# Element-wise work on SBUF operands moved from GpSimd to VectorE in a two-layer diffusion trunk

## The chip, the core and the metric

The program runs on one core of one Trainium2 chip, in one launch. The metric is the device time of one execution in microseconds, as a median over runs. The engines are TensorE (PE, matrix products), VectorE (DVE), ScalarE (ACT), GpSimd (POOL) and SyncE (SP, which only issues transfers). Each engine takes its own instructions strictly in order and waits on semaphores of the others.

## The reference: what is computed

Two layers of a trunk over 640 tokens (128 context tokens and 512 latent tokens) with 1024 channels, in float32. Each layer is: a normed and modulated copy of x, a token mixer, an output projection with a gated residual, a second norm, a SwiGLU feed-forward part of 2816 hidden units, and a second gated residual.

```python
for l in range(DEPTH):
    sh1, sc1, g1, sh2, sc2, g2 = split(silu(cond) @ ada_w[l] + ada_b[l], 6)
    h = rmsnorm(x, norm1_w[l]) * (1 + sc1) + sh1
    y, st = mixer_ab(h) if l % 2 == 0 else mixer_c(h)
    x = x + g1 * y
    h = rmsnorm(x, norm2_w[l]) * (1 + sc2) + sh2
    x = x + g2 * swiglu(h)
```

Layer 0's mixer is a chunked gated delta rule in two directions (convolution, SiLU and an l2 norm over q and k ahead of it, an RMS norm behind it) beside a grouped-query attention. Layer 1's mixer is a bidirectional chunked mLSTM. The states, the new keys and values, and y are returned.

## The kernel before

Activations lie transposed: 128 channels on the partitions, 640 tokens along the free axis, in 8 tiles. Every large product is made of three passes over fp32r operands: a number is split into a high part (a cast, on ACT) and a low part (the number less its high part), and the passes are high x high, high x low and low x high. So each weight block that arrives has a low part made once, and so has each activation tile.

The order of the work is this, with the times of the profiled execution:

- 0 to 60 us, `ada_start`: the modulation vectors of layer 0 come from row sums on DVE (`ada_tile`, L323). For each of 8 tiles of x a list (`START`) runs the row sums (`sc_in`), the sum of squares (`Norm.square`, L237) and the scaled split (`Norm.scale`, L217 to L223).
- 60 to 176 us, in `layer0`: 12 products `conv` (PE at L508, tile qkv). Behind each stand a 5-tap convolution on DVE (L980, four `scalar_tensor_tensor` on 644 elements), a SiLU on ACT (L984, tile kq or vy) and PE transposes of it (L992). Row sums of later modulation vectors (`ada_fill`, L323) are put in between. `Norm.finish` (L267, L269, L271) makes the normed activations, `bias_b` adds a bias to the gates and to z, and `after_k`, `after_q` make factors of the l2 norms.
- 176 to 430 us: the attention and the scan. `finish(c)` norms the output of each of five chunks.
- 412 to 500 us, `out_half` twice: 8 products of 24 matmuls each, the residual (`resid`, L558), and in the second one the scaled split and sum of squares of the next norm, with a spill of each tile by a DMA that POOL issues.
- 500 to 920 us: the feed-forward part of layer 0. 920 to 1264 us: `layer1`, which begins with two products on the raw activations (`gemm_pair`, tile mqk), `Norm.finish`, and the heads of q put into padded tiles (`qp`). After that come the projections of v and the gates (`gemm_tok`, L545), the mLSTM, its output projection, and the second feed-forward part until 1725 us.

`WStream.fetch` brings weight blocks: SP issues the transfer, ACT casts the high part (L483, tile wh), and the engine `W.eng` makes the low part (L484, tile wl, or wh where both parts share a slot). `W.eng` is POOL in the conv products, in layer 0's output projection and at the start of layer 1, and DVE elsewhere. `rsqrt` (L154) always runs on POOL, as a power with exponent -0.5.

The Python order gives priorities. A planner in the Tile framework then puts the instructions of each engine in order at build time, by data and by its own estimates of durations; on the chip that order is fixed.

Of the kernel before, what the change touches and what calls it, by code (L numbers as in the profile page):

```python
# [20 lines left out]
NK = 8  # L21
TP = 128
TS = 512
T = TP + TS
# [61 lines left out]
def tile_trunk(ctx: ExitStack, tc: tile.TileContext, A, dbg=None, stop=None):  # L86
# [101 lines left out]
    class Norm:  # L188
# [24 lines left out]
        def scale(self, k, x, eng=dve):  # L213
            h, sc = self.raw, self.sc
            v = None if eng is dve else t_tile("nv")[:, :T]
            for s, (a, b) in enumerate(SEG):
                act.activation((h.hi[k] if v is None else v)[:, a:b], x[:, a:b], AF.Copy, scale=sc(s, k))  # L217
                if v is None:
                    dve.scalar_tensor_tensor(out=h.lo[k][:, a:b], in0=x[:, a:b], scalar=sc(s, k),
                                             in1=h.hi[k][:, a:b].bitcast(F32), op0=ALU.mult, op1=ALU.subtract)  # L220
# [4 lines left out]
        def add(self, k, x, eng=dve):  # L225
            if self.raw:
                self.scale(k, x)
            self.square(k, x, eng)

        def square(self, k, x, eng=dve):  # L230
# [126 lines left out]
    def ada_start(nm):  # L357
# [15 lines left out]
        def x_in(k):  # L373
            sp.dma_start(out=xs[k], in_=A["x"][k])
            nm.square(k, xs[k], pool if k in (1, 3, 5, 7) else dve)
# [16 lines left out]
        def products(k):  # L392
# [3 lines left out]
            for t in range(NT):  # L396
# [6 lines left out]
              "s": lambda k: nm.scale(k, xs[k], pool if k in (1, 3, 5, 7) else dve)}  # L403
# [61 lines left out]
    class WStream:  # L465
        def __init__(self):
            self.i = 0
            self.eng = dve
# [3 lines left out]
        def fetch(self, depth):  # L472
            while len(self.ready) < depth and self.i < self.until:
# [10 lines left out]
                self.eng.tensor_tensor(out=lo, in0=raw[:, :n], in1=hi.bitcast(F32), op=ALU.subtract)  # L484
# [76 lines left out]
    def out_half(mx, xs, l, half, nm, js=range(NK), fill=0, eng=dve, spill=None):  # L561

        for j in js:
# [6 lines left out]
            if nm is not None:  # L570
                nm.add(j, xs[j], eng)
# [287 lines left out]
    def layer0(nm, accs, ws, xt, xs):  # L859
        with ExitStack() as lay:  # L860
# [73 lines left out]
            def bias_b():  # L934
# [5 lines left out]
                for t, n, b in ((slice(0, 1), 1, 0), (slice(1, NT), NT - 1, 272)):  # L940
                    pool.tensor_tensor(out=gat[:, t, :], in0=gat[:, t, :],
                                       in1=shw[:, None, b:b + 16].to_broadcast([P, n, 16]), op=ALU.add)
                    pool.tensor_tensor(out=zv[0][:, t, :], in0=zv[0][:, t, :],
# [59 lines left out]
            def after_k(hh):  # L1003
# [1065 lines left out]
```

## Time and profile before

| what | value |
|---|---|
| median of 3 runs | 1734.18 us (1732.96 to 1734.88) |
| the profiled execution's own time | 1727.01 us |
| its span, first to last instruction | 1725.1 us |
| PE busy | 1642.7 us, 95% of the span |
| DVE busy | 1242.5 us, 72% |
| ACT busy | 764.4 us, 44% |
| POOL busy | 268.4 us, 16% |
| mean granted TensorE clock | 0.989 of full speed |

The busy time of an engine includes the time for which an instruction has begun and is held up. The shares are averages over stages with very different limits, so stages are read by themselves: a view of windows gives the busy time of each engine in a stretch, the view of groups the mean duration of one instruction of a kind in that stretch, and the timeline single instructions with the idle time before them and what ended it.

### The profile page before, as it was taken

To read this page: it belongs to the slowest core of one execution; us is meant where nothing else is said; L and a number is where in the kernel's file an instruction comes from. 1 tells how busy PE (TensorE), PEld (TensorE's weight loads), DVE (VectorE), ACT (ScalarE), POOL (GpSimd) and SP (SyncE) were. 2 spreads that over 40 slices of the span, in tenths; PEclk is the share of its full clock that TensorE was granted. 3 is DMA by queue.
4 is the path that set the end of the run, shared out by engine and by line. 5 is a ranking of instruction groups with operands and counts; after the bars stand their busy time and mean duration, and the time that the engine had idled before them with its cause. 6 is when DMAs were issued, how large, how long until landed. Compare 5 with 4: busy or idle time off the path is not lost. (4 is left out here: it accounts for less than half of the span.)

```text
span 1725.1 us, 28119 instructions
## 1 busy us (share of the span) xinstructions
PE 1642.7 (95%) x10896; PEld 1565.6 (91%) x10896; DVE 1242.5 (72%) x2286; ACT 764.4 (44%) x1644; POOL 268.4 (16%) x318
## 2 busy tenths in 40 slices
PE   6888988998899999999999899999999999999998
PEld 3788876798899999999999889988999999999998
DVE  7798678778778889879755847457777988856432
ACT  5674256456364444442224423246455544434310
POOL 3344022663440000000002300001010000000000
PEclk9999999999999999999999999999999999999999
DMA  8233421104621444447633315411160344319321
GB/s 330 95 111 101 123 80 29 29 8 139 231 103 48 145 161 150 161 151 300 217 94 125 128 55 177 146 64 50 37 221 24 121 153 150 128 57 330 109 73 63
DMA packets 80653, 216.21 MB, mean 125 GB/s; under 512 B 20196, under 2 KB 21348, under 8 KB 80520
## 3 DMA queue, kind: packets, MB, share of 16 engines
q1 hardware_dynamic: 75720, 194.75, 34.0%
q0 software_dynamic: 4800, 19.66, 2.9%
q8 instruction: 86, 1.41, 0.3%
q14 instruction: 47, 0.39, 0.1%
HBM read 186.85 MB, written 27.53 MB: 124 GB/s over the span
## 5 line engine op out<-in xcount | busy, mean ns | idle before, releaser
L483 ACT CAST wh<-wr 128x1024 fp32r<-128x1024 f32 (+4 forms) x148 | 134.7, 914 | 296.2 <-DMA wr<-in_w_d 131.5
L508 PE MATMUL fd<-hid,wh 128*128 128x320 f32 x1408 | 264.4, 309 | 0.0
L508 PEld LDWEIGHTS fd<-hid,wh 128*128 128x128 f32 x1408 | 220.9, 188 | 0.3 <-ACT wh L483 0.3
L696 PE MATMUL sb<-ht,ph 128*128 128x320 f32 x1008 | 201.0, 313 | 3.8 <-DVE c L713 3.1
L484 DVE TENSOR_TENSOR wl<-wr,wh 128x1024 fp32r<-128x1024 f32 (+3 forms) x97 | 111.9, 1158 | 89.2 <-ACT wh L483 69.0
L696 PEld LDWEIGHTS sb<-ht,ph 128*128 128x128 f32 x1008 | 162.1, 190 | 6.6 <-DVE c L713 3.7
L508 PE MATMUL fd<-hid,wl 128*128 128x320 f32 x704 | 160.1, 309 | 1.4 <-DVE wl L484 1.4
L323 DVE SCALAR_TENSOR_TENSOR aj<-ar,cs 128x1024 bf16<-128x1024 f32 x112 | 133.6, 1219 | 24.4 <-DMA ar<-in_ada_w 24.2
L696 PE MATMUL sad<-hb,ph 128*128 128x320 f32 x576 | 128.4, 310 | 0.5 <-ACT sp L711 0.5
L508 PEld LDWEIGHTS fd<-hid,wl 128*128 128x128 f32 x704 | 117.9, 188 | 1.6 <-DVE wl L484 1.6
L508 PE MATMUL op<-mxh,wh 128*128 128x320 f32 x512 | 100.4, 314 | 7.3 <-DVE xb L558 5.1
L558 DVE SCALAR_TENSOR_TENSOR xd<-fd,mod,xd 128x128 f32<-128x128 f32 x96 | 48.4, 546 | 68.7 <-PE fd L508 68.6
L696 PEld LDWEIGHTS sad<-hb,ph 128*128 128x128 f32 x576 | 96.4, 188 | 1.1 <-ACT sp L711 1.1
L656 DVE TENSOR_TENSOR pl<-s,ph 128x1024 fp32r<-128x1024 f32 x72 | 88.0, 1222 | 4.1 <-ACT ph L655 3.6
L508 PEld LDWEIGHTS op<-mxh,wh 128*128 128x128 f32 x512 | 81.9, 191 | 8.7 <-ACT rh L217 5.3
L696 PE MATMUL sad<-hb,pl 128*128 128x320 f32 x288 | 89.0, 309 | 0.0
L696 PE MATMUL sb<-ht,pl 128*128 128x320 f32 x288 | 89.0, 309 | 0.0
L655 ACT CAST ph<-s 128x1024 fp32r<-128x1024 f32 x72 | 75.2, 1048 | 28.2 <-PE sad L696 9.2
L655 ACT CAST ph<-wp 128x1024 fp32r<-128x1024 f32 (+1 forms) x72 | 60.1, 835 | 41.4 <-PE sad L696 22.8
L824 POOL DMA_DIRECT2D hd<-c x18 | 9.8, 542 | 418.6 <-DVE c L823 418.6
L696 PE MATMUL sad<-ht,ph 128*128 128x320 f32 x288 | 64.9, 312 | 1.6 <-DVE c L707 1.4
L656 DVE TENSOR_TENSOR pl<-wp,ph 128x1024 fp32r<-128x1024 f32 x36 | 43.9, 1221 | 29.1 <-issue 21.1
(559 smaller groups left out, 4203.1 us busy)
## 6 DMA issues: line engine op xcount, KB each, us to landing
ar<-in_ada_w SPq DMA_DIRECT2D x61, 512.0 KB
wp<-in_w_g SPq DMA_DIRECT2D x36, 512.0 KB
wp<-in_w_u SPq DMA_DIRECT2D x36, 512.0 KB
wr<-in_w_d SPq DMA_DIRECT2D x32, 512.0 KB
hf<-hd SPq DMA_DIRECT2D x44, 320.0 KB
hd<-c POOLq DMA_DIRECT2D x36, 320.0 KB, 2.6
adas<-in_ada_w SPq DMA_DIRECT2D x19, 512.0 KB
wr<-in_w_ml SPq DMA_DIRECT2D x20, 416.0 KB
```

Source lines behind the costliest of these rows:

```text
L323: dve.scalar_tensor_tensor(out=junk, in0=st, scalar=one, in1=ada["cs"][:, s, :], op0=ALU.mult, op1=ALU.mult, accum_out=mod[l][q][:, s, j:j ...
L483: act.copy(hi, raw[:, :n])
L484: self.eng.tensor_tensor(out=lo, in0=raw[:, :n], in1=hi.bitcast(F32), op=ALU.subtract)
L508: pe.matmul(ps[:, LO + a:LO + b], lhsT=wv[:, k, :], rhs=xk[:, a:b], start=k == 0 and p_ == 0, stop=k == kk - 1 and p_ == 2)
L558: dve.scalar_tensor_tensor(out=x[:, a:b], in0=ps[:, LO + a:LO + b], scalar=gate[:, s, j:j + 1], in1=x[:, a:b], op0=ALU.mult, op1=ALU.add)
L655: act.copy(hi, src)
L656: dve.tensor_tensor(out=lo, in0=src, in1=hi.bitcast(F32), op=ALU.subtract)
L696: pe.matmul(bank[o], lhsT=wv[:, k, :], rhs=xv, start=o not in seen and k == 0 and p_ == 0, stop=k == 3 and p_ == 2, skip_group_check=True)
L824: pool.dma_start(out=hd[f], in_=c1)
```

## The change: what it does

POOL keeps the powers of `rsqrt`, its memsets, its DMA issues and the inversion of small triangular blocks. Everything else that it computed in the places below goes to DVE, and in two places the form changes:

- `WStream.fetch`: the low parts of weights are always made on DVE. This moves 34 instructions: 16 of 1024 elements, 15 of 512 and 3 of 832.
- `Norm.square`: 11 additions of 640 elements, 4 in `ada_start` and 7 in the second `out_half`.
- `Norm.scale` for odd tiles in `ada_start`: POOL's path (two scalings to a buffer and a cast on ACT, one subtraction on POOL) becomes the path of even tiles (two scalings on ACT that write the high part, two `scalar_tensor_tensor` on DVE). Four casts on ACT fall away.
- `bias_b`: four additions, the largest of 1024 elements.
- `after_k`, `after_q`: seven operations on 20 or 40 elements, each of which stands behind POOL's power.
- `finish(c)`: one product of 4 elements for each of five chunks, behind POOL's power.
- `layer1`, j < 2: two products of 640 elements go to DVE, and the eight scalings into `qp` go to ACT, as for j = 2 and 3.

```diff
         def scale(self, k, x, eng=dve):
-            v = None if eng is dve else t_tile("nv")[:, :T]
             for s, (a, b) in enumerate(SEG):
-                act.activation((h.hi[k] if v is None else v)[:, a:b], x[:, a:b], AF.Copy, scale=sc(s, k))
-                if v is None:
-                    dve.scalar_tensor_tensor(out=h.lo[k][:, a:b], ...)
-            if v is not None:
-                act.copy(h.hi[k][:, :T], v)
-                eng.tensor_tensor(out=h.lo[k][:, :T], in0=v, in1=h.hi[k][:, :T].bitcast(F32), op=ALU.subtract)
+                act.activation(h.hi[k][:, a:b], x[:, a:b], AF.Copy, scale=sc(s, k))
+                dve.scalar_tensor_tensor(out=h.lo[k][:, a:b], in0=x[:, a:b], scalar=sc(s, k),
+                                         in1=h.hi[k][:, a:b].bitcast(F32), op0=ALU.mult, op1=ALU.subtract)
...
-                eng.tensor_tensor(out=self.acc, in0=self.acc, in1=sq, op=ALU.add)
+                dve.tensor_tensor(out=self.acc, in0=self.acc, in1=sq, op=ALU.add)
...
-                self.eng.tensor_tensor(out=lo, in0=raw[:, :n], in1=hi.bitcast(F32), op=ALU.subtract)
+                dve.tensor_tensor(out=lo, in0=raw[:, :n], in1=hi.bitcast(F32), op=ALU.subtract)
...
-                    pool.tensor_tensor(out=gat[:, t, :], ...)
+                    dve.tensor_tensor(out=gat[:, t, :], ...)
-                    pool.tensor_tensor(out=zv[0][:, t, :], ...)
+                    dve.tensor_tensor(out=zv[0][:, t, :], ...)
...
                     rsqrt(rk, ssk)
-                    pool.tensor_tensor(out=nk, in0=ssk, in1=rk, op=ALU.mult)
-                    pool.tensor_tensor(out=rk2, in0=rk, in1=rk, op=ALU.mult)
+                    dve.tensor_tensor(out=nk, in0=ssk, in1=rk, op=ALU.mult)
+                    dve.tensor_tensor(out=rk2, in0=rk, in1=rk, op=ALU.mult)
...
                     rsqrt(rq, ssq)
-                    pool.tensor_scalar(out=rq, in0=rq, scalar1=128.0 ** -0.5, scalar2=None, op0=ALU.mult)
-                    pool.tensor_tensor(out=rq2, in0=rq, in1=rq, op=ALU.mult)
+                    dve.tensor_scalar(out=rq, in0=rq, scalar1=128.0 ** -0.5, scalar2=None, op0=ALU.mult)
+                    dve.tensor_tensor(out=rq2, in0=rq, in1=rq, op=ALU.mult)
...
                 rsqrt(rs, so)
-                pool.tensor_tensor(out=rs, in0=rs, in1=rq[:, c, :], op=ALU.mult)
+                dve.tensor_tensor(out=rs, in0=rs, in1=rq[:, c, :], op=ALU.mult)
...
-                (pool if j < 2 else dve).tensor_tensor(out=y[:, :T], in0=src[:, :T], in1=nm.bc[:, :T], op=ALU.mult)
+                dve.tensor_tensor(out=y[:, :T], in0=src[:, :T], in1=nm.bc[:, :T], op=ALU.mult)
...
-                        if j < 2:
-                            pool.tensor_scalar(out=qp[2 * j + i][r, a:b], ...)
-                        else:
-                            act.activation(qp[2 * j + i][r, a:b], y[r, a:b], AF.Identity, scale=0.125, ...)
+                        act.activation(qp[2 * j + i][r, a:b], y[r, a:b], AF.Identity, scale=0.125, ...)
```

The other lines of the diff drop the names `W.eng` and `eng`.

## Rows read from the trace of the kernel before

**Rows 1.** Windows: stretch and length, then each engine's busy us (instructions), clock, DMA.

```profile
9.00:49.00 40.00, 32.18 (x140) 16.96 (x138) 36.39 (x46) 21.20 (x37) 14.95 (x7) 1.00 0.80 316
84.00:146.00 62.00, 49.70 (x316) 48.44 (x316) 59.41 (x91) 43.16 (x118) 32.83 (x15) 0.91 0.33 111
146.00:176.00 30.00, 30.00 (x194) 29.52 (x195) 25.35 (x50) 12.61 (x36) 7.18 (x4) 0.93 0.29 91
460.00:500.00 40.00, 34.95 (x227) 34.72 (x226) 35.85 (x50) 22.19 (x34) 24.65 (x20) 0.96 0.43 151
950.00:973.00 23.00, 17.97 (x121) 17.25 (x119) 21.02 (x34) 11.61 (x21) 12.42 (x15) 0.93 0.25 88
```

**Rows 2.** Waits of PE, 60 to 176 us: total us, times, longest.

```profile
PE tr L992 <- ACT kq L984: 12.3, 4, 6.3
PE qkv L508 <- ACT hh L269: 4.9, 1, 4.9
```

**Rows 3.** Timeline of PE: start, us, instruction, idle before it and what ended it.

```profile
474.55 0.48 PE L508 MATMUL op<-mxh,wh 128*128 128x320 f32 x1 [5.05 <-DVE xb L558]
...
972.93 0.72 PE L545 MATMUL tkm<-wl,hh 128*128 128x416 f32 x1 [3.97 <-POOL v L1541]
```

**Rows 4.** Timeline of DVE in two places.

```profile
134.83 3.02 DVE L980 SCALAR_TENSOR_TENSOR cy<-cbuf,cw,cy 128x644 f32<-128x644 f32 x1
...
144.13 0.89 DVE L980 SCALAR_TENSOR_TENSOR cy<-cbuf,cw,cy 128x644 f32<-128x644 f32 x1
...
468.07 4.47 DVE L211 TENSOR_TENSOR rl<-mod,rh 128x4 fp32r<-128x4 f32 x3
...
472.65 0.17 DVE L211 TENSOR_TENSOR rl<-mod,rh 128x4 fp32r<-128x4 f32 x1
```

**Rows 5.** Timeline of POOL in two places.

```profile
133.77 9.64 POOL L484 TENSOR_TENSOR wl<-wr,wh 128x1024 fp32r<-128x1024 f32 x3
...
970.56 2.32 POOL L484 TENSOR_TENSOR wl<-wr,wh 128x832 fp32r<-128x832 f32 x1 [8.16 <-DVE nu L267]
```

**Rows 6.** Groups of POOL, whole span: shapes, count, busy us, mean ns, idle before.

```profile
L484 POOL TENSOR_TENSOR wl<-wr,wh 128x1024 fp32r<-128x1024 f32 x16 | 43.0, 2701 | 57.3 <-ACT wh L483 53.1 <-PE fd L508 4.2
...
L484 POOL TENSOR_TENSOR wh<-wr,wh 128x512 fp32r<-128x512 f32 x15 | 20.8, 1400 | 32.8 <-ACT wh L483 32.8
...
L154 POOL TENSOR_TENSOR ors<-so,mhalf 128x4 f32<-128x4 f32 x5 | 5.0, 1008 | 26.4 <-ACT jk L1421 22.4 <-ACT wh L483 4.0
...
L154 POOL TENSOR_TENSOR rk<-ssk,mhalf 128x20 f32<-128x20 f32 x1 | 4.2, 4187 | 5.8 <-DVE one L336 5.8
```

**Rows 7.** Groups of DVE, 9 to 49 us.

```profile
L323 DVE SCALAR_TENSOR_TENSOR adaj<-ads,cs 128x1024 bf16<-128x1024 f32 x16 | 24.7, 1543 | 3.0 <-ACT cs L302 2.6
L237 DVE TENSOR_TENSOR nacc<-nacc,nsq 128x640 f32<-128x640 f32 x3 | 4.6, 1519 | 1.7 <-ACT nsq L236 0.9 <-ACT sc L382 0.8
```

**Rows 8.** Groups of DVE, 84 to 146 us.

```profile
L980 DVE SCALAR_TENSOR_TENSOR cy<-cbuf,cw,cy 128x644 f32<-128x644 f32 x24 | 35.7, 1498 | 2.4 <-ACT cy L978 2.2
L323 DVE SCALAR_TENSOR_TENSOR adaj<-adas,one,cs 128x1024 bf16<-128x1024 f32 x13 | 20.9, 1606 | 0.1
```

**Rows 9.** Timeline of ACT at the start of layer 1.

```profile
967.39 0.87 ACT L483 CAST wh<-wr 128x832 fp32r<-128x832 f32 x1
```

**Rows 10.** Groups of DVE, whole span.

```profile
L323 DVE SCALAR_TENSOR_TENSOR aj<-ar,cs 128x1024 bf16<-128x1024 f32 x112 | 133.6, 1219 | 24.4 <-DMA ar<-in_ada_w 24.2
...
L484 DVE TENSOR_TENSOR wl<-wr,wh 128x1024 fp32r<-128x1024 f32 x62 | 76.8, 1243 | 48.0 <-ACT wh L483 34.2 <-PE fd L508 8.0 <-ACT nms L245 5.5
...
L795 DVE TENSOR_TENSOR hid<-hf,hid 128x640 fp32r<-128x640 f32 x44 | 35.5, 820 | 8.5 <-ACT hid L794 8.0
...
L484 DVE TENSOR_TENSOR wl<-wr,wh 128x832 fp32r<-128x832 f32 x17 | 17.4, 1023 | 19.1 <-ACT wh L483 12.6 <-ACT og L1561 6.3
...
L484 DVE TENSOR_TENSOR wh<-wr,wh 128x512 fp32r<-128x512 f32 x17 | 11.7, 688 | 6.6 <-ACT wh L483 6.6
...
L1094 DVE SCALAR_TENSOR_TENSOR an<-aq,ars,qw 128x128 f32<-128x128 f32 x20 | 6.0, 349 | 4.5 <-POOL ars L154 4.5
```

More of the change, by code (lines that the diff above doesn't have):

```diff
@@ L211, in shift, with scale, add, square @@
                 dve.tensor_tensor(out=lo, in0=sh[:, 2 * i:2 * i + 2], in1=hi.bitcast(F32), op=ALU.subtract)
-        def scale(self, k, x, eng=dve):
+        def scale(self, k, x):
             h, sc = self.raw, self.sc
-            v = None if eng is dve else t_tile("nv")[:, :T]
             for s, (a, b) in enumerate(SEG):
-                act.activation((h.hi[k] if v is None else v)[:, a:b], x[:, a:b], AF.Copy, scale=sc(s, k))
-                if v is None:
-                    dve.scalar_tensor_tensor(out=h.lo[k][:, a:b], in0=x[:, a:b], scalar=sc(s, k),
-                                             in1=h.hi[k][:, a:b].bitcast(F32), op0=ALU.mult, op1=ALU.subtract)
-            if v is not None:
-                act.copy(h.hi[k][:, :T], v)
-                eng.tensor_tensor(out=h.lo[k][:, :T], in0=v, in1=h.hi[k][:, :T].bitcast(F32), op=ALU.subtract)
-        def add(self, k, x, eng=dve):
+                act.activation(h.hi[k][:, a:b], x[:, a:b], AF.Copy, scale=sc(s, k))
+                dve.scalar_tensor_tensor(out=h.lo[k][:, a:b], in0=x[:, a:b], scalar=sc(s, k),
+                                         in1=h.hi[k][:, a:b].bitcast(F32), op0=ALU.mult, op1=ALU.subtract)
+        def add(self, k, x):
             if self.raw:
                 self.scale(k, x)
-            self.square(k, x, eng)
-        def square(self, k, x, eng=dve):
+            self.square(k, x)
+        def square(self, k, x):
             if self.acc is None:
@@ L374, in x_in @@
             sp.dma_start(out=xs[k], in_=A["x"][k])
-            nm.square(k, xs[k], pool if k in (1, 3, 5, 7) else dve)
+            nm.square(k, xs[k])
         def sc_in(k):
@@ L402, in ada_start @@
         do = {"w": sc_in, "x": x_in, "n": sh_in, "W": W.fetch, "t": products,
-              "s": lambda k: nm.scale(k, xs[k], pool if k in (1, 3, 5, 7) else dve)}
+              "s": lambda k: nm.scale(k, xs[k])}
         stats = nm.stats()
@@ L559, in resid, with out_half @@
                                      in1=x[:, a:b], op0=ALU.mult, op1=ALU.add)
-    def out_half(mx, xs, l, half, nm, js=range(NK), fill=0, eng=dve, spill=None):
+    def out_half(mx, xs, l, half, nm, js=range(NK), fill=0, spill=None):
         for j in js:
@@ L570, in out_half @@
             if nm is not None:
-                nm.add(j, xs[j], eng)
+                nm.add(j, xs[j])
             if spill is not None:
@@ L940, in bias_b @@
                 for t, n, b in ((slice(0, 1), 1, 0), (slice(1, NT), NT - 1, 272)):
-                    pool.tensor_tensor(out=gat[:, t, :], in0=gat[:, t, :],
+                    dve.tensor_tensor(out=gat[:, t, :], in0=gat[:, t, :],
                                        in1=shw[:, None, b:b + 16].to_broadcast([P, n, 16]), op=ALU.add)
-                    pool.tensor_tensor(out=zv[0][:, t, :], in0=zv[0][:, t, :],
+                    dve.tensor_tensor(out=zv[0][:, t, :], in0=zv[0][:, t, :],
                                        in1=shw[:, None, b + 16:b + 272].to_broadcast([P, n, 256]), op=ALU.add)
@@ L1525, in layer1 @@
                     for s, (a, b) in enumerate(SEG):
-                        if j < 2:
-                            pool.tensor_scalar(out=qp[2 * j + i][r, a:b], in0=y[r, a:b], scalar1=0.125,
-                                               scalar2=bias[r, 2 * j + s:2 * j + s + 1], op0=ALU.mult, op1=ALU.add)
-                        else:
-                            act.activation(qp[2 * j + i][r, a:b], y[r, a:b], AF.Identity, scale=0.125,
-                                           bias=bias[r, 2 * j + s:2 * j + s + 1])
+                        act.activation(qp[2 * j + i][r, a:b], y[r, a:b], AF.Identity, scale=0.125,
+                                       bias=bias[r, 2 * j + s:2 * j + s + 1])
             nm.raw.put()
             U.put(nm.bc)
-            W.eng = dve
             gt = sm([NT, 32], "gt")
@@ L1910, in tile_trunk @@
     W.fetch(2)
-    W.eng = dve
     mneg = v3(t_tile("mneg")[:, :2 * P], 2)
@@ L1919, in tile_trunk @@
     ada_open()
-    W.eng = pool
     out_half(mx, xs, 0, 1, None, fill=(0, 1, 0, 1, 0, 1, 0, 1))
@@ L1924, in tile_trunk @@
     xd, xf = (dram.tile([NK, P, T], F32, name=n) for n in ("xd", "xf"))
-    out_half(mx, xs, 0, 0, nm, fill=(1, 0, 0, 0, 0, 0, 0, 0), eng=pool, spill=xf)
+    out_half(mx, xs, 0, 0, nm, fill=(1, 0, 0, 0, 0, 0, 0, 0), spill=xf)
     ada_fill(max(0, len(ada_todo) - 56))
@@ L1928, in tile_trunk @@
     mx.put()
-    W.eng = dve
     def done0(j, x):
```

8 lines of the change are left out of this document (2 added, 6 removed).

## The prediction

> **What bounds the kernel now.** I read the page first: PE is busy for 95% of the span, so over most of it nothing that DVE or POOL does matters, and a change of these engines is worth something only where PE stands still or slows. The idle time of PE on the timeline and in the waits says where that is near the edits. Between 60 and 176 us PE waits 12.3 us in four waits for a SiLU'd convolution (three of them over 1.5 us, the longest 6.3) and 4.9 us for the normed activations [rows 2]; at 474.55 it has waited 5.05 us for a residual on DVE, and at 972.93 3.97 us [rows 3]. That row names a memset on POOL, but the memset follows the low part of a weight block, 970.56 + 2.32 = 972.88 [rows 5], and the matmul reads that low part. Behind such a wait the granted clock dips: its mean is 0.91 from 84 to 146 us and 0.93 from 950 to 973 [rows 1], so part of PE's work then runs at the lower level.
>
> Then the windows: who is full where PE waits? DVE, with 36.39 of 40 us, 59.41 of 62, 35.85 of 40 and 21.02 of 23 [rows 1]. And the timelines of DVE and POOL side by side say what fills it. A convolution step that takes 0.89 us at 144.13 takes 3.02 us at 134.83 [rows 4], while POOL makes three low parts from 133.77 on [rows 5]. Two things that were meant to run side by side take turns.
>
> Here the Trainium skill bears (SBUF — State Buffer, Who interferes with whom): a DVE instruction with two SBUF inputs and a GpSimd instruction that reads SBUF share one read interface, and the second to start waits for the whole of the first. The stretched rows agree: 3.02 less 0.89 is 2.13 us, most of one low part on POOL.
>
> **The change part by part.** Times are against the profiled execution's own 1727.01 us (span 1725.1); the median of the runs, 1734.18, is 7.2 above it, and I add 7.2 at the end. Each stage is a ledger for DVE: stretches that go, instructions that come, waits that come.
>
> *9 to 49 us.* The 16 row sums took 1543 ns on average [rows 7], where the same kind takes 1219 elsewhere [rows 10]: 16 x 0.32 = 5.2 us go. The three additions took 1519 instead of 820 (640 elements) [rows 7, 10]: 2.1 go. What comes: four additions at 0.82 = 3.3, and four pairs of `scalar_tensor_tensor`, together 640 elements each, some 0.2 more than 0.82 for the second instruction: 4.1. That is +0.1, so 0. Above, each added addition may wait behind ACT's square, as the three did (1.7/3 = 0.57 each): +2.3. Below, four ACT casts fall away, and the last low part of x no longer goes through them: -1.5 at most, an estimate of one cast (0.87 [rows 9]) and half an addition.
>
> *60 to 84 us.* Two splits and four additions of the gates; the wait of 4.9 us is for ACT [rows 2], which works through the gates' functions, and covers them. 0; if that cover is gone, +1; if the gates start earlier by the stretch of one POOL instruction, -2.
>
> *84 to 146 us, the largest term.* 24 convolution steps of 1498 ns instead of 890 [rows 8, 4]: 14.6 us go. 13 row sums of 1606 instead of at most 1280 (1219 [rows 10] and some 60 for a scalar from a tile): 4.2 go. Nine of the twelve splits of the products fall here, 9 x 1.22 = 11.0 come (1243 with some stretch [rows 10]); five small operations of about 0.17 (a 4-element one [rows 4]) = 0.9 come. They stand behind POOL's power of 20 elements, 4.19 us [rows 6], and DVE, in order, stands too: the next convolution steps and row sums are queued behind them, and the SiLU and PE's transposes wait for those. How much of 4.19 the planner covers with other DVE work is unknown: all, or nothing. The nearest row is DVE behind the powers of the attention's norms, 4.5 us over five waits [rows 10], 0.9 each although such a power takes 1 us or more [rows 6]; so about 1.1 is covered, and I take 3.1. Sum -18.8 + 11.0 + 0.9 + 3.1 = -3.8. Low: the wait covered, -6.9, and the clock's dips smaller, say -8. High: the full wait, and each split waits for ACT's cast as the 62 on DVE do on average (34.2/62 = 0.55 [rows 10], 9 x 0.55 = 5.0): +2.3.
>
> *146 to 176 us.* One split, two small operations and the power for q: 1.2 + 0.3 + 3.1 = 4.6 come, nothing goes. DVE is idle for 4.65 of these 30 us, but PE is never [rows 1], and the convolutions feed it just in time. A third passes: +1.5. Ends: 0 (all in DVE's idle time) and +4.6.
>
> *396 to 430 us.* Five products behind powers of 1.01 us [rows 6]. With 1.1 covered they cost nothing; the cover is the other direction's scan on DVE. Without it 5 x 1.0 = +5. Six splits of 0.69 [rows 10] come, about as much as the stretches that go with POOL's: 0.
>
> *430 to 500 us.* Some nine splits of 512 (6.2), two of 1024 (2.4) and seven additions (5.7) come, 14.3; I count no gain over the stage, since PE is fed through most of it. What can be read is the wait of 5.05: the residual stood behind three tiny operations that took 4.47 us where one alone takes 0.17 [rows 3, 4], so 4.0 of it was POOL's turn. In place of that come an addition and a 1024 split, 0.82 + 1.22 = 2.0 [rows 10]. -2.0. Low: all 5.05. High: in the second half DVE has per tile a residual and a scaled split (about 1.05 each, as the pairs above), an addition (0.82) and a split (0.69), 3.6 us or 28.8 for eight tiles, which fits into a stretch of 40; but four of the first half's splits may come in the way of a residual, 4 x 0.69: +2.8.
>
> *935 to 980 us.* The low part ended at 972.88 on POOL [rows 5]. Its cast ended at 967.39 + 0.87 = 968.26 [rows 9]. On DVE it takes 1.02 [rows 10] and its priority is that of an early fetch; with the mean wait of 0.55 and a place behind one running instruction (0.75) it ends near 970.6, so -2.3; PE's clock behind a shorter wait may give back more. Ends: -4.0 and 0. The eight scalings into `qp` come on ACT, which is half idle (11.61 of 23 [rows 1]): 0.
>
> *Sum:* 0 + 0 - 3.8 + 1.5 + 0 - 2.0 - 2.3 = -6.6. The execution comes to 1720.4, the median to **1727.6 us**.
>
> **The rivals.**
>
> *It is a swap and nothing moves.* For: what goes in the ledgers and what comes are near each other (18.8 against 15.0 from 84 to 146; 7.3 against 7.4 at the start), and PE's 95% leaves little. Against: the named waits end in a stretch. Time: within 3.4 of before, 1733. The Trainium skill's advice (Perfetto Trace Analysis, Optimizing Scalar/DVE Operations) says the same: since the two share a read port, moving work between them might not help.
>
> *DVE stands behind POOL's powers and ACT's casts (the slower case).* A power has no cover and splits wait in line: +2.3 (84 to 146) + 4.6 + 5.0 - 2.0 - 2.3 + 2.3 (start) = +9.9, 1744. For: DVE is in order and already waits on POOL and ACT in [rows 10]. Against: the waits there are short, and a planner orders around what it expects. It decides when more than about 6 of the 13.4 us of powers (4.19 + 4.15, taken as equal, + 5 x 1.01) stand open.
>
> *Everything closes.* All waits of rows 2 and 3 but the one for ACT's gates go, 12.3 + 5.05 + 3.97 = 21.3: 1713. For: the planner reckons without the taking of turns, and with one engine its order fits the chip. Against: DVE stays full from 84 to 146.
>
> *It does not do what it says:* the planner's new order undoes a stage that the diff does not touch. Either sign, a few us; no row bears on it.
>
> **How the numbers follow.** Below 0.2% (3.5 us) a measurement of this kernel can't tell a change from none. Forecast (1721 to 1731) 0.43; everything closes 0.10; swap 0.20; slower 0.22; a foreign reordering 0.05, split evenly. Faster 0.54, same 0.21, slower 0.25. The low ends sum to about -20 (-1.5 - 2 - 8 - 5 - 4), 1714; the high ends to +18, and not all come at once; 1 in 10 above the slower case's 1744. Range 1714 to 1744.
>
> **What would show it.** Right: from 84 to 146 us the convolution steps average near 0.89 and no row is over 1.3; PE's wait for kq falls from 12.3 to under 8; the waits at 474.55 and 972.93 are halved; POOL's busy time falls by over 100 us; DVE shows two waits of 2 to 4 us on the powers rk and rq. Wrong: DVE's idle time behind POOL's power or ACT's cast over 10 us in all, or PE's waits moved to 146 to 176 us, or stretched DVE rows with POOL idle.

## The result, and the profile after

The changed kernel takes **1704.62 us** (median of 4 runs, 1703.51 to 1706.11) against 1734.23 us for the kernel before (4 runs): a ratio of 0.9831, 95% interval 0.9814 to 0.9848, or 29.6 us less. The prediction was 1727.6 us with a range of 1714 to 1744. The direction was right; the time lies 9 us below the range. The profiled execution took 1704.41 us, with a span of 1702.6 us.

The busy line of the page: PE works as long as before, POOL 115.6 us less, and DVE, which took over POOL's work, is not busier but 15.8 us less busy, since the time for which its instructions were held up counted as busy.

```profile
PE 1641.7 (96%) x10896; PEld 1564.8 (92%) x10896; DVE 1226.7 (72%) x2357; ACT 762.9 (45%) x1646; POOL 152.8 (9%) x243
```

The windows over the stretches that hold the work of [rows 1] (stretch and length, busy us and instructions of PE, PEld, DVE, ACT, POOL, then granted clock, DMA share, GB/s). From 84 to 146 us PE had stood for 12.3 us; in the same work it now stands for 3.9 of 51. In the 40 us shown of the output projection it stands for nothing.

```profile
8.00:48.00 40.00, 35.97 (x145) 17.42 (x144) 35.83 (x58) 22.43 (x40) 0.00 (x0) 0.96 0.84 327
79.00:130.00 51.00, 47.12 (x317) 45.80 (x318) 46.64 (x102) 40.48 (x116) 4.50 (x1) 0.99 0.39 125
130.00:160.00 30.00, 28.24 (x191) 27.96 (x190) 27.32 (x53) 12.43 (x37) 4.10 (x1) 0.97 0.40 123
440.00:480.00 40.00, 40.00 (x274) 40.00 (x273) 36.91 (x73) 22.68 (x35) 4.54 (x8) 1.00 0.57 191
931.00:954.00 23.00, 20.93 (x130) 20.42 (x129) 20.99 (x44) 16.27 (x31) 0.83 (x4) 0.94 0.44 143
```

The waits of PE from 60 to 160 us (total us, times, longest), against 12.3 and 4.9 in [rows 2]:

```profile
PE tr L986 <- ACT kq L978: 3.4, 2, 2.3
PE tr L986 <- ACT vy L978: 1.8, 1, 1.8
PE qkv L502 <- DVE hl L266: 1.6, 1, 1.6
```

Of the two rows of PE's timeline in [rows 3] the first has no successor (0.2 us of waiting for a residual are left from 410 to 471 us); the second is this one, half as long:

```profile
950.70 0.46 PE L539 MATMUL tkm<-wl,hh 128*128 128x416 f32 x1 [2.07 <-DVE wl L478]
```

The groups of DVE from 79 to 130 us answer to [rows 8], and those from 8 to 48 us to [rows 7] (count, busy us, mean ns, idle before). A convolution step takes 885 ns instead of 1498, a row sum 1282 and 1220 instead of 1606 and 1543.

```profile
L974 DVE SCALAR_TENSOR_TENSOR cy<-cbuf,cw,cy 128x644 f32<-128x644 f32 x23 | 19.8, 885 | 0.0
L318 DVE SCALAR_TENSOR_TENSOR adaj<-adas,one,cs 128x1024 bf16<-128x1024 f32 x11 | 14.1, 1282 | 0.0
L478 DVE TENSOR_TENSOR wl<-wr,wh 128x1024 fp32r<-128x1024 f32 x7 | 8.5, 1220 | 0.0
...
L318 DVE SCALAR_TENSOR_TENSOR adaj<-ads,cs 128x1024 bf16<-128x1024 f32 x16 | 19.5, 1220 | 2.8 <-ACT cs L297 2.6
```

The waits of DVE from 79 to 160 us: the two that the prediction expected, of the size that it expected.

```profile
DVE nk L1009 <- POOL rk L154: 3.4, 1, 3.4
DVE rq L1021 <- POOL rq L154: 2.2, 1, 2.2
```

By marks that both traces have (the first matmul of a product), the changed kernel is 0.9 us ahead at the first q product, 16.4 when z's product begins, 11.5 at the first output transpose of the scan, 19.6 when the feed-forward part begins, 19.0 at layer 1, 22.9 behind its start stage, and 22.5 at the end.

### The profile page after: what moved, and what is told of

It reads as the page before. It is cut to its first block, busy times and chain, and to the rows that moved or that the text cites. A ratio compares the mean times of both kernels' runs of the same rounds, so it can differ in the third digit from the quotient of the medians.

```text
span 1702.6 us, 28080 instructions
## 1 busy us (share of the span) xinstructions
PE 1641.7 (96%) x10896; PEld 1564.8 (92%) x10896; DVE 1226.7 (72%) x2357; ACT 762.9 (45%) x1646; POOL 152.8 (9%) x243
## 4 chain that ended last, share of the span: by engine, by line
PE 79%; DVE 8%; ACT 5%; DMA 3%; POOL 2%; issue 2%; SPq 0%; DVEq 0%; ACTq 0%; POOLq 0%
PE fd L502 18%; PE sb L690 13%; PE sad L690 10%; PE op L502 5%; PE tka L539 3%; PE fg L502 3%; PE tkb L539 3%; PE fu L502 3%; PE qkv L502 3%; PE mqk L502 3%; PE tkm L539 2%; PE mw L1328 1%; PE apo L1280 1%; DVE adaj L318 1%; POOL ars L154 1%
## 5 line engine op out<-in xcount | busy, mean ns | idle before, releaser
L478 DVE TENSOR_TENSOR wl<-wr,wh 128x1024 fp32r<-128x1024 f32 (+3 forms) x116 | 133.0, 1151 | 93.1 <-ACT wh L477 74.1
L649 ACT CAST ph<-wp 128x1024 fp32r<-128x1024 f32 (+1 forms) x72 | 60.0, 835 | 41.6 <-PE sad L690 22.9
L650 DVE TENSOR_TENSOR pl<-wp,ph 128x1024 fp32r<-128x1024 f32 x36 | 43.9, 1220 | 29.0 <-issue 21.0
L690 PE MATMUL sb<-hn,ph 128*128 128x320 f32 x288 | 64.8, 309 | 0.0
```

Source lines behind the costliest of these rows:

```text
L478: dve.tensor_tensor(out=lo, in0=raw[:, :n], in1=hi.bitcast(F32), op=ALU.subtract)
L649: act.copy(hi, src)
L650: dve.tensor_tensor(out=lo, in0=src, in1=hi.bitcast(F32), op=ALU.subtract)
L690: pe.matmul(bank[o], lhsT=wv[:, k, :], rhs=xv, start=o not in seen and k == 0 and p_ == 0, stop=k == 3 and p_ == 2, skip_group_check=True)
```

## The experiments

Each part alone first, then what POOL does to DVE, then the products behind the powers. Times are medians; a difference is against the kernel before in the same comparison (1731.5 to 1733.0 us) unless another is named.

**The conv splits alone.**

```diff
             rk = sm([NT, 4], "rk")
-            W.eng = pool
```

> The kernel before with one part alone: the weight splits of layer 0's q, k, v and z products subtract on VectorE instead of GpSimd. The whole change was 29.6 us faster (1734.2 to 1704.6), and between the two traces 16.4 us of it had been won when z's product began. Theory A (GpSimd's element-wise work on operands in SBUF holds VectorE up, the order that was planned does not allow for it, and so PE waits at the k and q transposes and runs on at the half clock behind each wait): this part alone brings most of the 16.4, 8 to 14 us; PE's idle time between 60 and 176 us falls from 17.2 to under 9 us, and the time at the half clock there from 17 to under 8 us. Theory B (GpSimd's splits are merely late, 2.4 us against 1.2, and TensorE waits for the low parts themselves): also faster, but by the waits that name a split, under 4 us. Theory C (it is the new order of instructions that came out better, by chance): anything between -8 and +8, and no fewer waits of PE at the k and q transposes.

Measured: 1717.65 us, ratio 0.991 (0.9893 to 0.9928), -14.8 us, 0.8 more than theory A's highest case. All four waits for kq are gone; what PE still waits for from 60 to 180 us is this:

```profile
PE qkv L508 <- ACT hh L269: 3.9, 1, 3.9
PE qkv L508 <- DVE hl L271: 0.4, 1, 0.4
PE tr L992 <- ACT vy L984: 0.2, 1, 0.2
```

The windows from the first q product to z's product, the kernel before and then this one:

```profile
60.00:176.36 116.36, 99.16 (x631) 96.37 (x631) 106.86 (x177) 72.20 (x179) 48.03 (x25) 0.93 0.31 101
```

```profile
62.80:160.92 98.12, 93.64 (x627) 91.86 (x627) 92.24 (x183) 68.92 (x176) 17.56 (x13) 0.97 0.36 119
```

The stretch is 18.2 us shorter. PE's idle time in it goes from 17.2 to 4.5 us, 12.7 less. The part of the time lost to the lower clock goes from 0.07 x 116.36 = 8.1 to 0.03 x 98.12 = 2.9 us, 5.2 less; PE's busy time for the same matmuls falls by 5.5. Together 17.9. DVE's groups in the same two stretches, before and this kernel:

```profile
L980 DVE SCALAR_TENSOR_TENSOR cy<-cbuf,cw,cy 128x644 f32<-128x644 f32 x44 | 53.7, 1225 | 4.5 <-ACT cy L978 4.1
L323 DVE SCALAR_TENSOR_TENSOR adaj<-adas,one,cs 128x1024 bf16<-128x1024 f32 x18 | 27.3, 1517 | 0.3
...
L484 DVE TENSOR_TENSOR wl<-wr,wh 128x1024 fp32r<-128x1024 f32 x2 | 2.5, 1226 | 0.1
```

```profile
L980 DVE SCALAR_TENSOR_TENSOR cy<-cbuf,cw,cy 128x644 f32<-128x644 f32 x40 | 35.0, 884 | 0.2
L323 DVE SCALAR_TENSOR_TENSOR adaj<-adas,one,cs 128x1024 bf16<-128x1024 f32 x18 | 23.0, 1280 | 0.0
L484 DVE TENSOR_TENSOR wl<-wr,wh 128x1024 fp32r<-128x1024 f32 x14 | 17.0, 1225 | 1.4 <-ACT wh L483 1.4
```

What goes: 44 x 0.341 + 18 x 0.237 = 19.3 us of stretch, and 3.4 in the small shapes of hl and nu, 22.7. What comes: 14.5 us of splits. Net -8.2, near the -7.4 of the prediction's ledger. But four convolution steps and a scaling of v, 4.6 us, now also lie behind the beginning of z's product. -8.2 - 4.6 = -12.8 comes near the 12.7 of PE's idle time; that they agree to 0.1 us is luck, for by the windows DVE is busy 14.6 us less and idle 3.6 less. The clock is the rest. Theory A holds for the waits; theory B's waits (PE on a low part) do not occur in either stretch.

**The output projections alone, and the start of layer 1 alone.**

```diff
     ada_open()
-    W.eng = pool
...
-    out_half(mx, xs, 0, 0, nm, fill=(1, 0, 0, 0, 0, 0, 0, 0), eng=pool, spill=xf)
+    out_half(mx, xs, 0, 0, nm, fill=(1, 0, 0, 0, 0, 0, 0, 0), spill=xf)
```

> The kernel before with one part alone: in the two output projections of layer 0 the weight splits, and in the second half also the low parts and the sums of squares of the next norm, run on VectorE instead of GpSimd. Between the traces of before and after this stage gained about 7 us (the mark at its last tile went from -12.8 to -19.6). Theory A: it brings 4 to 8 us alone; the wait of PE at 474.55 (5.05 us) is gone. Theory C (order by chance): between -3 and +3, and a wait of 3 us or more stays somewhere in the stage. Had the prediction been right in this stage: -2.0.

Measured: 1722.0 us, ratio 0.9937 (0.9922 to 0.9952), -10.4 us, 2.4 more than theory A's highest case. The windows of the two projections, first a second profile of the kernel before and then this kernel:

```profile
430.00:493.40 63.40, 57.98 (x366) 57.73 (x367) 49.75 (x83) 25.61 (x39) 31.20 (x24) 0.92 0.56 190
```

```profile
429.50:483.20 53.70, 52.38 (x355) 51.90 (x354) 47.60 (x99) 24.82 (x39) 4.02 (x7) 1.00 0.66 226
```

Idle time falls from 5.4 to 1.3 us, and 0.08 x 63.4 = 5.1 us of lost clock go: 9.2 in all, the clock more than half of it (in the first profile of before the clock took 0.03 x 60.25 = 1.8). DVE holds 16 instructions more and is busy 2.1 us less.

```diff
             ys = []
-            W.eng = pool
...
-                (pool if j < 2 else dve).tensor_tensor(out=y[:, :T], in0=src[:, :T], in1=nm.bc[:, :T], op=ALU.mult)
+                dve.tensor_tensor(out=y[:, :T], in0=src[:, :T], in1=nm.bc[:, :T], op=ALU.mult)
...
-                        if j < 2:
+                        if True:
```

> The kernel before with one part alone: at the start of layer 1 the weight splits and the products of the first two q/k tiles run on VectorE and their scaled copies on ScalarE, instead of on GpSimd. Between the two traces this stage gained 3.9 us. Theory A: -2 to -4.5 us; the wait of PE at 972.93 (3.97 us) is gone. Theory C: between -1 and +2. Predicted for this stage: -2.3.

Measured: 1725.26 us, ratio 0.996 (0.9943 to 0.9976), -7.2 us, more than any theory gave. In its trace PE's wait is 2.08 us instead of 3.97, as in the changed kernel, and the stage from mqk to the bc of layer 1 is 4.1 us shorter. The other 3 us were not found in a stage, and executions of one kernel differ by as much (the second profile of the kernel before, below).

**The start stage and the additions of the gates.**

```diff
-            nm.square(k, xs[k], pool if k in (1, 3, 5, 7) else dve)
+            nm.square(k, xs[k], dve)
...
-              "s": lambda k: nm.scale(k, xs[k], pool if k in (1, 3, 5, 7) else dve)}
+              "s": lambda k: nm.scale(k, xs[k], dve)}
...
-                    pool.tensor_tensor(out=gat[:, t, :], ...)
-                    pool.tensor_tensor(out=zv[0][:, t, :], ...)
+                    dve.tensor_tensor(out=gat[:, t, :], ...)
+                    dve.tensor_tensor(out=zv[0][:, t, :], ...)
```

> The kernel before with two parts alone: the odd tiles' squares and low parts in the start stage, and the additions of the shift rows to the gates and z, run on VectorE instead of GpSimd. The parts run so far sum to -20.4 us, the whole is -29.6. If parts simply add: -9. By the traces (the first q product starts 0.9 us earlier in the changed kernel, and z's stage is as long as before) these two bring 0 to -1.5, and the missing 8 us then lie in how the small products and the splits meet on GpSimd.

Measured: 1726.54 us, ratio 0.9963 (0.9951 to 0.9974), -5.5 us, between the two values expected. Its two halves were run by themselves.

> The kernel before with one part alone: the odd tiles' squares and low parts of the start stage on VectorE. With the additions of the gates it brought 5.5 us. If the start stage does it: 1728 to 1730, and the first q product begins about 2.5 us earlier than in other kernels that leave this stage alone (60.5 to 61.9 us there). If the two parts only act together, or it is the additions: 1731 to 1734.

> The kernel before with one part alone: the additions of the shift rows to the gates and z (640 and 40 elements) on VectorE. If they bring about half of the 5.5 us: 1729 to 1731, by stretches that go from VectorE's work between 60 and 90 us (GpSimd is busy 3.7 us with them). If they bring nothing, as predicted: 1731 to 1734.

Measured: the start stage 1727.63 us (0.9976, 0.9964 to 0.9988), -3.9 us; the additions 1728.7 us (0.9985, 0.9973 to 0.9997), -2.8 us, the latter barely more than the 0.14% by which a copy of the kernel before differed from itself (below), so that it is not shown by this run; the fastest kernel shows it (below). With the start stage moved, the first q product begins at 58.24 us; in the kernels that leave it alone this was at 59.1 to 62.1. The prediction had 0 for both. It took PE's wait of 4.9 us in [rows 2] for ScalarE's own work; with the additions on DVE what is left of it is 2.0 us.

**What on POOL holds DVE up.** The kernel with the conv splits on DVE gets the load on POOL back, as instructions whose output nobody reads: one behind each split of the conv stage, a subtraction in the first run and a power in the second.

```diff
+                if self.dummy:
+                    pool.tensor_tensor(out=raw[:, :n], in0=raw[:, :n], in1=hi.bitcast(F32), op=ALU.subtract)
...
+                    pool.tensor_tensor(out=raw[:, :12], in0=ones[:, :12], in1=hi[:, :12].bitcast(F32), op=ALU.pow)
```

> The kernel with the conv splits on VectorE (1717.7 us) and, behind each of those splits, one more subtraction of the same operands (128x1024, fp32) on GpSimd, written over the raw weights; nobody reads what it writes. Theory A (GpSimd's work on SBUF operands holds VectorE up while it runs): the gain is given back, +12 to +25 us against that kernel; the mean of VectorE's conv steps rises from under 1.0 to over 1.3 us, and PE waits again for the k and q rows in front of their transposes. Theory B (low parts made on GpSimd come late): no low part comes from GpSimd here, so within 2 us of 1717.7. Theory C (the order of the instructions): within 4 us of 1717.7, and the conv steps stay under 1.0 us.

> The same as the run with the second subtraction, but the extra operation of GpSimd is a power of 12 elements per partition, which by the powers of the trace (20 elements in 4.15 us, 4 in 1.0 us) lasts about 2.5 us, as long as the subtraction of 1024 elements, and reads and writes 1 in 85 of the data. Theory A in the form that the traffic of GpSimd's operands holds VectorE up: within 3 us of 1717.7, conv steps under 1.0 us. Theory A in the form that GpSimd's being busy at all does it: +12 to +25 us, as the subtractions. Theory C (an additional operation of GpSimd changes the planned order): the same as the subtractions do.

Measured: 1737.64 us with the subtractions (+20.0 against 1717.65), 1725.79 with the powers (+8.1). The conv steps average 1246 ns with the subtractions, somewhat under the 1.3 us expected, and PE waits for kq again, 9.3 us in five waits. The conv steps of DVE, 60 to 180 us, and POOL's extra instructions, first with subtractions, then with powers:

```profile
L983 DVE SCALAR_TENSOR_TENSOR cy<-cbuf,cw,cy 128x644 f32<-128x644 f32 x39 | 48.3, 1246 | 0.2
...
L487 POOL TENSOR_TENSOR wr<-wr,wh 128x1024 f32<-128x1024 f32 x12 | 35.6, 2978 | 55.1 <-DVE wl L485 26.9 <-DVE cbuf L979 13.9 <-PE tr L995 7.3
```

```profile
L983 DVE SCALAR_TENSOR_TENSOR cy<-cbuf,cw,cy 128x644 f32<-128x644 f32 x48 | 42.2, 885 | 6.1 <-ACT cy L981 5.8
...
L487 POOL TENSOR_TENSOR wr<-cm,wh 128x12 f32<-128x12 f32 x12 | 32.6, 2725 | 50.8 <-DVE wl L485 31.9 <-DVE cbuf L979 13.8 <-ACT wh L484 5.1
```

The stretch is there with the one and not with the other, with POOL as busy. But the powers cost 8 us as well, and the waits of ACT in their run say why: the write into the raw weights keeps that buffer until POOL's queue has come round, and the next cast stands in front of ACT's SiLU.

```profile
ACT wh L484 <- POOL wr L487: 11.2, 4, 8.1
```

So both were run again with a scratch buffer for the output, and a third time with the subtraction on DVE.

```diff
-                    pool.tensor_tensor(out=raw[:, :n], in0=raw[:, :n], ...)
+                    pool.tensor_tensor(out=W.scr[:, :n], in0=hi.bitcast(F32), in1=hi.bitcast(F32), op=ALU.subtract)
...
+                    pool.tensor_tensor(out=W.scr[:, :12], in0=ones[:, :12], in1=hi[:, :12].bitcast(F32), op=ALU.pow)
...
+                    dve.tensor_tensor(out=W.scr[:, :n], in0=hi.bitcast(F32), in1=hi.bitcast(F32), op=ALU.subtract)
```

> The kernel with the conv splits on VectorE, and behind each split one more subtraction of 128x1024 on GpSimd, this time from the rounded weights into a scratch buffer of its own, so that no raw buffer is held until GpSimd is done (in the first pair of runs ScalarE's casts waited 6.8 and 11.2 us for that). Theory A (GpSimd's traffic on SBUF operands holds VectorE up): +10 to +16 us against 1717.7, about the 11.9 us by which the subtractions were slower than the powers; conv steps over 1.2 us on average. Theory C (order): under +4, conv steps under 1.0.

> The same with powers of 12 elements per partition into the scratch buffer. If the 8 us that the first powers cost came from the raw buffers held by GpSimd's queue: within 3 us of 1717.7, and ScalarE's casts wait for no GpSimd operation. If GpSimd's being busy, or one more operation in the planned order, costs by itself: +5 to +11 again. Conv steps under 1.0 us by either.

> The same with the extra subtraction of each weight block on VectorE itself: every conv split is done twice there, 15 more instructions of 1.22 us, 18.3 us. The prediction charged such splits to the path in full where VectorE was full: then nine of them lie between 84 and 146 us, +11 us or more against 1717.7. Theory D (VectorE has row sums to fill its time with that nobody waits for soon; what the plan knows of is put into their place, and only the stretches that it does not know of fall on the steps that PE waits for): under +4 us, and fewer of the 1024-element row sums between 60 and 176 us than the 23 of the kernel without the extra splits.

Measured: 1733.28 us with subtractions on POOL, 1717.97 with powers on POOL, 1727.53 with subtractions on DVE. With POOL's subtractions the conv steps average 1071 ns, less than the 1.2 us expected. The same view for the three, in this order:

```profile
L983 DVE SCALAR_TENSOR_TENSOR cy<-cbuf,cw,cy 128x644 f32<-128x644 f32 x42 | 44.7, 1071 | 0.1
L323 DVE SCALAR_TENSOR_TENSOR adaj<-adas,one,cs 128x1024 bf16<-128x1024 f32 x18 | 29.4, 1631 | 0.0
L485 DVE TENSOR_TENSOR wl<-wr,wh 128x1024 fp32r<-128x1024 f32 x14 | 20.4, 1464 | 1.2 <-ACT vy L987 1.0 <-ACT wh L484 0.2
...
L487 POOL TENSOR_TENSOR scr<-wh 128x1024 f32<-128x1024 f32 x12 | 29.0, 2413 | 52.1 <-ACT wh L484 51.8
```

```profile
L983 DVE SCALAR_TENSOR_TENSOR cy<-cbuf,cw,cy 128x644 f32<-128x644 f32 x48 | 42.2, 886 | 0.2
...
L487 POOL TENSOR_TENSOR scr<-cm,wh 128x12 f32<-128x12 f32 x12 | 33.1, 2762 | 37.0 <-ACT wh L484 36.7
```

```profile
L983 DVE SCALAR_TENSOR_TENSOR cy<-cbuf,cw,cy 128x644 f32<-128x644 f32 x44 | 38.4, 883 | 2.1 <-ACT cy L981 2.1
...
L487 DVE TENSOR_TENSOR scr<-wh 128x1024 f32<-128x1024 f32 x12 | 14.7, 1221 | 1.1 <-ACT wh L484 1.1
```

PE's waits for kq, from 60 to 180 us, with subtractions and then with powers on POOL; the first is close to the 12.3 in four of [rows 2]:

```profile
PE tr L995 <- ACT kq L987: 11.6, 4, 5.9
```

```profile
PE tr L995 <- ACT kq L987: 0.2, 1, 0.2
```

This settles what it is. POOL busy for 33.1 us with powers costs nothing (1717.97 against 1717.65) and stretches nothing; busy for 29.0 us with subtractions it costs 15.3 us more, and conv steps, row sums and DVE's own splits are all longer. It is the operands' traffic, and neither POOL's being busy nor one more instruction in the planned order. Theory C falls: in these two traces all 10896 instructions of PE, the 1642 of ACT and the 318 of POOL stand in the same order, and so do the 2298 of DVE, but for two pairs of neighbours that begin within 4 ns of each other. Theory B falls too: with the low parts made on DVE, but POOL's subtractions kept, the time is that of the kernel before (1733.0). Whether it is what POOL reads or what it writes that holds DVE up was not separated.

Theory D holds for the stage and not for the kernel. The extra instructions on DVE are 12, 14.7 us, and not the 15 of the expectation. With 10 of them on DVE by then, z's product begins only 2.3 us later than with the powers, since four conv steps, three splits and a row sum fewer have run. They come due beside z's product, where PE waits 3.5 us for a low part, and by the first output of the scan another 8.9 us are paid. In all the 14.7 us cost 9.6. With POOL's subtractions nothing could be put off, since the order is the same, and z's product begins 15.5 us later: the stretch of conv steps, row sums and splits up to 180 us, 7.8 + 6.3 + 3.4 = 17.5 us, costs 15.3. The difference between planned work and unplanned stretch is one of degree.

**The products behind the powers.** Those named rk2, bU, sK, rq and rq2 go the same way as nk.

```diff
-                    pool.tensor_tensor(out=nk, in0=ssk, in1=rk, op=ALU.mult)
+                    dve.tensor_tensor(out=nk, in0=ssk, in1=rk, op=ALU.mult)
...
-                pool.tensor_tensor(out=rs, in0=rs, in1=rq[:, c, :], op=ALU.mult)
+                dve.tensor_tensor(out=rs, in0=rs, in1=rq[:, c, :], op=ALU.mult)
```

> The kernel before with one part alone: the small products behind the powers of the k and q norms, and the product behind the power in the scan's output norm, run on VectorE instead of GpSimd, so that VectorE now waits for GpSimd's powers. Between the two traces the scan (z's product to the first output transposes) lost 4 to 5 us, and VectorE's waits for the powers of rk and rq were 3.4 and 2.2 us. If the waits cost the path what they last: +4 to +8 us. If the scan's loss is what else changed (order, the slower clock): within 1.5 us of before. If the products on GpSimd had held VectorE up as the splits did: -1 to -3.

Measured: 1744.43 us, ratio 1.0067 (1.0046 to 1.0088), +12.0 us, more than the highest case. DVE's timeline at the k norm (start, us, instruction, idle before):

```profile
132.84 2.35 DVE L1015 TENSOR_TENSOR nk<-ssk,rk 128x20 f32<-128x20 f32 x1 [3.45 <-POOL rk L154]
135.12 2.37 DVE L1016 TENSOR_TENSOR rk<-rk 128x20 f32<-128x20 f32 x1
```

DVE waits 3.45 us for the power, and as soon as it is there POOL goes on with the splits that it had in its queue (4.68 us from 132.78), and each product of 20 elements, which takes 0.18 us otherwise, is held for over 2 us. DVE is out for 8 us, and PE's longest wait for kq from 60 to 180 us is 9.2 us. This part, taken back in the changed kernel, makes the fastest version. First all of these products go back to POOL, then only the one of the scan:

> The changed kernel with the small products behind the powers (k and q norms, and the scan's output norm) put back on GpSimd, so that VectorE does not wait for the powers. In the kernel before these products moved alone cost 12 us. If that price also holds here, where GpSimd has no splits left to do: 1692 to 1695. If the price came mostly from the splits that GpSimd had still to do: 1697 to 1702 (the scan's 4 to 5 us come back, and the waits of 3.4 and 2.2 us at the k and q norms were hidden). If the products do not matter in this setting: 1703 to 1706.

> The changed kernel with only the product behind the power of the scan's output norm back on GpSimd. With all the small products back the time was 1692.3, 12.4 us less than the changed kernel; by the marks of the two traces 5.7 us of that had come when z's product began (the k and q norms) and another 5 in the scan. So 1697 to 1701 if the two groups simply add; 1692 to 1694 if the scan's product alone did it; 1703 to 1706 if the k and q norms did.

Measured: **1692.26 us** with all of them on POOL (1691.79 to 1694.19; ratio to the kernel before 0.9768, 0.9751 to 0.9785), 12.4 us less than the changed kernel; 1699.46 with only the scan's (ratio 0.9806, 0.9779 to 0.9834), 5.2 us less. So 5.2 us are the scan's and the other 7.2 fall to the k and q norms; these were not put back alone, so that the two add is not shown by itself, but the traces bear it out, where the stretch from the first q product to z's product is 5.6 us shorter with all of them back than in the changed kernel. The waits of PE, 60 to 180 us, in the fastest kernel, where those for kq sum to 1.3, and then the waits of DVE for the scan's powers in the changed kernel (330 to 430 us):

```profile
PE qkv L502 <- DVE hl L266: 1.6, 1, 1.6
PE tr L986 <- ACT kq L978: 1.3, 2, 1.1
```

```profile
DVE ors L1418 <- POOL ors L154: 5.1, 5, 1.2
```

The last experiment on the fastest kernel puts the additions of the gates back on POOL:

> The fastest kernel so far (the change, with the small products behind the powers back on GpSimd: 1692.3) with the additions of the shift rows back on GpSimd too. If those additions hold VectorE up: 1694 to 1697. If it matters only that VectorE has fewer instructions: 1690 to 1692. No difference: 1691.5 to 1693.5.

Measured: 1697.54 us (ratio 0.9808, 0.9791 to 0.9824), 5.3 us slower than the fastest kernel, a little over the highest case. PE's one wait ahead of the products on the normed activations, 1.6 us there, is 3.8 again; where the rest of the 5.3 us lies is open.

**The kernel before once more.**

> The kernel before, unchanged, for a second profile. The first profiled execution took 1727.0 us, the median of its runs is 1732 to 1734. If executions differ in a stage: the profile shows where, by the marks; the kernels that leave the start stage alone began their first q product 0.1 to 2.9 us later than the first profile, so 1.5 to 3 us of it are expected there, and the rest in the feed-forward stages. If the profiled execution is as fast as the first one again: 1726 to 1728, and profiling shifts the time.

Measured: 1733.61 us against 1731.5 for the same code in the same comparison (ratio 1.0014, 1.0005 to 1.0023), which is what this measurement can't tell from no change. The profiled execution took 1732.8 us, and its busy line, for comparison with the 1642.7 us of PE in the first profile, is this:

```profile
PE 1649.2 (95%) x10896; PEld 1572.1 (91%) x10896; DVE 1241.9 (72%) x2286; ACT 764.8 (44%) x1644; POOL 268.7 (16%) x318
```

When z's product begins it is 0.4 us behind the first profile; 2.3 us are lost between the scan's first output and the feed-forward part, and 4.1 between the down products of layer 0 and layer 1. In the output projection the idle time is the same (5.4 and 5.7 us) but the mean clock is 0.92, where it was 0.97 from 430 to 490.25 us in the first profile. So executions differ by how long the clock stays low behind the same waits: between the two profiles PE's idle time is the same (82.4 and 81.7 us), and its busy time is not.

## Why the prediction was wrong

The parts alone, beside what the prediction's terms gave them:

| part | predicted | measured alone |
|---|---|---|
| start stage | 0 | -3.9 |
| additions of the gates | 0 | -2.8 (not clear of noise) |
| conv splits (-18.8 + 11.0 + 0.4) | -7.4 | -14.8 |
| products behind powers (0.9 + 3.1 + 1.1 + 0) | +5.1 | +12.0 |
| output projections | -2.0 | -10.4 |
| start of layer 1 | -2.3 | -7.2 |
| sum | -6.6 | -27.1 (the whole: -29.6) |

*The mechanism was right.* POOL's subtractions of 1024 elements stretched DVE's steps, and the stretch went: 1498 to 885 ns. The signs of "what would show it" came: the wait at 474.55 went but for 0.2 us, the one at 972.93 to 52%, and the two waits of DVE had the size named. One sign of "wrong" came with them: DVE's idle time behind POOL's powers is 3.4 + 2.2 + 5.1 = 10.7 us, over the 10 that were named. The Trainium skill's rule (SBUF — State Buffer, Who interferes with whom) agrees for the subtractions: 1071 against 886 ns with the same DVE work. Its advice that moving work between the two engines might not help (Perfetto Trace Analysis, Optimizing Scalar/DVE Operations), which the rival of the swap leaned on, does not hold here: the three parts that move subtractions of weights won 14.8, 10.4 and 7.2 us.

*The step that failed is the sum of the stages: it took the net of DVE's ledger for what PE gains, and the clock for a constant.* The -6.6 is idle time of PE alone. Between the two traces that idle time fell from 1725.1 - 1642.7 = 82.4 to 1702.6 - 1641.7 = 60.9 us, by 21.5, 14.9 more than forecast. Two stages hold most of it: from the first q product to z's product it fell by 10.2 us, where the ledger had 2.3 (-3.8 + 1.5), and from the first output of the scan to the feed-forward part by 7.2, where it had 2.0. The other 8 of the 23.0 us between 1727.6 and 1704.6 are time at the lower clock: PE's busy time fell by 1.0 between the two traces, and 7.0 are the forecast's offset.

*The net of the ledger was near and its use was wrong.* With the conv splits alone it was -8.2 from 60 us to z's product, against -7.4. But the prediction took the splits of the last stretch for a cost (+0.4 of 1.2), where work of 4.6 us could slip beside z's product, and it let the output projection keep 3 of its 5.05 us for the addition and the split that come in their place, where all but 0.2 went.

*The clock stood at nothing in the sum.* "PE's clock behind a shorter wait may give back more" stood in the text, [rows 1] had the clock at 0.91 and 0.93, and only the low end from 84 to 146 us held something for it (-6.9 to -8). In the conv stage 5.2 us of the 17.9 are the clock, in the output projections 5.1 of 9.2 (1.8 by the first profile).

*The offset was the clock too.* 7.2 us were added between a profiled execution and the median. But that execution, at a mean clock of 0.989, lost about 0.011 x 1725.1 = 19 us to the lower clock, and the 70 executions of the kernel before in the experiments, at 0.985 on average, lost about 26. So the 7 us are time at the lower clock, and the change took as much away: the four executions of the changed kernel, at 0.988 to 0.992, lost about 16, and its profiled execution lies at its median. With -22.5 in place of -6.6 the forecast would still have come out at 1711.7, 7 us high.

*The powers were underpriced,* +5.1 for 12.0. The waits had about the sizes forecast, 3.4 and 2.2, and in the changed kernel the stage of the k and q norms lost 5.6 us, near the 5.1. In the scan, "With 1.1 covered they cost nothing" was wrong: five waits of 1.0 stood open and cost 5.2 us. The trace of before had a sign of it: in the attention DVE waited 0.62 to 0.88 us behind each of five powers of 0.70 us, so that little or nothing of them was covered. What the 12.0 in the kernel before holds beyond that begins with products held beside POOL's splits (2.35 and 2.37 us). Of 13.4 us of powers 10.7 stood open, more than the 6 from which the slower rival was to decide. That rival's mechanism was there; it lost because the rest won more than its price.

*The low end* of the range was the sum of the parts' low ends. Four of six parts came out below the low end of their own (-4 from 935 to 980, -5.05 in the projection, -1.5 at the start, -2 at the gates), and the conv splits below the -8 of their stage. "Everything closes", 1713, had part of the cause and the smallest chance of the worked-out rivals; the measured time lies below even that, though waits of 3.4 us for kq and of 2.07 at the start of layer 1 stayed, since other idle time and the clock came on top.

## What to carry to other kernels

Price a wait of the bounding engine with what follows it: read the granted clock behind the wait and add what is lost there, at the low end of the range above all. A profiled execution that is faster than the median may owe that to its clock; then the difference is no constant to be added to a forecast. Time in which an engine is held up by another is not quite a load like an instruction, since the planned order makes no room for it: here 17.5 us of stretch cost 15.3, and 14.7 us of planned instructions 9.6. When work moves off an engine, leave there what stands behind that engine's own slow instruction: here the small products behind the powers gave back 12 us of the 40 that the rest had won.

## What the runs showed of the hardware

Powers on POOL held DVE up by nothing: 12 of 2762 ns each, reading operands in SBUF, left the conv steps at 886 ns, where subtractions of 2413 ns made them 1071, with the same order of instructions on every engine. The Trainium skill (SBUF — State Buffer, Who interferes with whom) calls what the two engines share an exclusive lock, and has a DVE instruction with two SBUF inputs contend with a GpSimd instruction that reads SBUF; for a POOL instruction with little data these rows show no hold at all. A product of 20 elements on DVE, 0.18 us otherwise, took 2.35 us beside POOL's subtractions.

The price of a power goes up with its elements, 2.7 us for 12 and 4.15 for 20, but not by them alone: 4 elements took 1.0 us in the scan [rows 6] and 2.0 in the attention, and why is open.

```profile
L154 POOL TENSOR_TENSOR ars<-ass,mhalf 128x4 f32<-128x4 f32 x5 | 10.0, 1993 | 72.7 <-DVE ass L1090 72.7
...
L154 POOL TENSOR_TENSOR ars<-ass,mhalf 128x2 f32<-128x2 f32 x5 | 3.5, 698 | 13.5 <-DVE ass L1090 13.5
```

And the same waits of PE cost a different time from one execution to the next, by the clock behind them: in the output projections of the kernel before the mean clock was 0.97 in one execution and 0.92 in another, with 5.7 and 5.4 us of idle time.
